# Heads' gate rows of an mLSTM mixer spread over the partitions by a stride-zero transfer in place of a product with a selection column

## The chip, the cores and the metric

The kernel runs on one core of a Trainium2 chip. The metric is the device time of one execution in microseconds (us). TensorE (PE in the profile, PEld its weight loads) multiplies matrices into PSUM; VectorE (DVE), ScalarE (ACT) and GpSimd (POOL) do the rest; SyncE (SP) issues most transfers. SBUF and PSUM have 128 partitions. A time between two kernels is called different here from about 0.2% on.

## The reference, cut to what matters

One layer of a streaming encoder, for a prompt of 2048 tokens and a sample of 64: adaLN and RMSNorm, one input projection, a causal pooling mixer beside an mLSTM with four heads, an output projection, and then a gated MLP. The part that the change touches is the weight matrix of the mLSTM within one chunk of tokens:

```python
b = jnp.cumsum(lf, -1)
dmat = b[..., :, None] - b[..., None, :] + ig[..., None, :]
dmat = jnp.where(causal, dmat, -jnp.inf)
m_t = jnp.maximum(b + m[..., None], dmat.max(-1))
wt = jnp.exp(dmat - m_t[..., None])
a = wt * jnp.einsum('bhtd,bhsd->bhts', q, k)
```

For each head, `wt[t, s]` is the exponential of a term that depends on `t` alone (`b[t] - m[t]`) plus a term that depends on `s` alone (`ig[s] - b[s]`), masked to `s <= t`. The kernel works in chunks of 128 tokens of the prompt (and 64 of the sample).

## The kernel before, in words

The tokens stand in four groups (`groups`, `o.g` 0 to 3) of 512; the last one, `o.last`, also holds the 64 of the sample. For each group the kernel runs the projections of `v` and the gates (`proj_v`), for each of four heads the projections q, k and the output gate (`proj_qko`, 24 matmuls of 512 columns each), four projections for pooling, and the output projection. After the four groups the MLP follows, from about 760 us to the end. Weights are split by ScalarE (line 392) and VectorE (line 395) into a rounded part and a remainder, and each product takes three passes.

The small work between the projections is written as generators. `gemm` calls `tick(0)` after some of its matmuls, which runs the first generator of a list one `yield` further. Two of them matter here. `gate_rows` makes, from the gates, four rows `r` (head by token, on 4 partitions: the term of `t`), a table `R4` and from it, transposed, the columns `CL` (the terms by token on the partition); `drain(0)` in the main loop finishes it before the first `lstm` of the group. `lstm` runs once per head. Its first step builds `at`, the matrix `wt` times the products of k and q:

- line 1274: PE spreads row `hd` of `r` over the partitions, as a product of `E_r[:, hd]` (a selection column, broadcast to 128 columns) with `RHL`. `RHL` holds `r` twice, as a rounded part on partitions 0 to 3 and as the remainder on 32 to 35, since the product reads its operands in a rounded type;
- ScalarE takes the exponential of that PSUM row plus the column of `CL`, four tiles of 128 x 128 into `at`; VectorE clips it by the mask;
- line 1287: PE transposes k, and VectorE multiplies it by a column of `CL` into `kw`;
- line 1297: PE multiplies k and q, and VectorE multiplies `at` by the result.

The second step multiplies `kw` with `va` (line 1312); the third multiplies q with the state (1332) and `at` with `va` (1334).

The order of the instructions on each engine is drawn up by the framework when the kernel is compiled, from the order of the program and simulated times. What is issued through `Urgent` is ranked as if it had been written 200 instructions earlier. `keep_in_program_order` places an instruction behind the one written before it on the same engine. In the profile an instruction issued through `Urgent` has line 231, so that tiles tell more than lines there. Each engine runs its queue in order; a transfer is issued on the queue of an engine, and if it has to wait, what stands behind it waits too. In group 0 VectorE also works through reductions of the conditioning weights (`ada`, line 208).

The kernel already had one transfer of the new kind: `ada` spreads rows of `cs`, in DRAM, over 128 partitions (`s<-cs`, `u<-cs`, `acc<-cs`, line 200), issued by SyncE.

Of the kernel before, what the change touches and what calls it, by code (L numbers as in the profile page):

```python
# [9 lines left out]
F32 = mybir.dt.float32  # L10
F32R = mybir.dt.float32r
# [5 lines left out]
P = 128  # L17
# [23 lines left out]
NH = 4  # L41
# [23 lines left out]
def tile_layer(ctx: ExitStack, tc: tile.TileContext, xT, vecs, cst, rst, w_mod, w_ada, c_rows, w_qkou, w_v, w_pool,  # L65
# [21 lines left out]
    def m2_ps():  # L87
        return bank("m2")
# [34 lines left out]
    def extra():  # L123
        while side:
            try:
                next(side[0])
                return
            except StopIteration:
                side.pop(0)
# [688 lines left out]
    if True:  # L818
# [270 lines left out]
        E_r = a1.tile([P, NH], F32R, tag="E_r", name="E_r")  # L1089
        R4 = a1.tile([P, TMAX], F32, tag="R4", name="R4")  # L1090
        pool.memset(R4, 0.0)
        RHL = a1.tile([P, TMAX], F32R, tag="RHL", name="RHL")
        pool.memset(RHL.bitcast(F32), 0.0)
# [59 lines left out]
        def gate_rows(o, gt, cols):  # L1153
# [55 lines left out]
            act.activation(RHL[0:4, :T], r[:4, :T], AF.Copy)  # L1209
            dve.tensor_tensor(out=RHL[32:36, :T], in0=r[:4, :T], in1=RHL[0:4, :T].bitcast(F32), op=ALU.subtract)  # L1210
            for _ in range(8):
                yield

# [20 lines left out]
            cols += [CL, GL]  # L1234
# [25 lines left out]

        ends = []

        def lstm(o, hd, qko, va, cols, mix):
# [3 lines left out]
            CL, GL = cols  # L1267
            at = a2.tile([P, TMAX], F32, tag="at", name="at")
            kw = a2.tile([P, 5, P], F32, tag="kw", name="kw", bufs=1)
            nd = a2.tile([P, 5, 129], F32, tag="nd", name="nd")  # L1270
            for (a, b, n, s) in o.tsegs:
                lo, w = a * P, (b - a) * n
                pr = m2_ps()
                pe.matmul(pr[:n, :w], E_r[:, hd:hd + 1].broadcast_to([P, n]), RHL[:, lo:lo + w], start=True, stop=True)
                for ti in range(a, b):
                    c0 = (ti - a) * n
                    act.activation(at[:n, ti * P:ti * P + n], pr[:n, c0:c0 + n], AF.Exp, bias=CL[:n, ti, 0, hd:hd + 1])

                av = at[:n, lo:lo + w].rearrange("p (t c) -> p t c", c=n)
                dve.tensor_tensor(out=av, in0=av, in1=mask[:n, :n].unsqueeze(1).broadcast_to([n, b - a, n]), op=ALU.min)  # L1280
# [22 lines left out]
            extra()  # L1303
            yield
# [131 lines left out]
        for o in groups:  # L1436
# [16 lines left out]
            if o.g == 0:  # L1453
                t = scr()
                nc.sync.dma_start(out=t[:P, :NH], in_=cst[:P, NCST + 512:NCST + 512 + NH])
                dve.tensor_copy(E_r, t[:P, :NH])
# [757 lines left out]
def _constants():  # L2214
    c = np.zeros((P, NCST + 512 + NH), np.float32)
# [8 lines left out]
    for h in range(NH):  # L2224
        c[h, NCST + 512 + h] = c[32 + h, NCST + 512 + h] = 1.0
# [71 lines left out]
```

## Time and profile before

| | |
|---|---|
| median of 3 runs | 2172.56 us (2170.78 to 2175.88) |
| the profiled execution | 2170.94 us |
| its span, first to last instruction | 2169.1 us |
| mean granted TensorE clock | 0.998 |
| attention stage | up to about 760 us |
| products of line 1274 | 20, modelled duration 6.6 us in all |
| bytes moved by the transfers | 543.63 MB |

A row of a timeline has the start in us, the us from there to the end of a merged run, the engine, the line, the operation, the tile written and the tiles read, shapes, and the count; brackets at its end give the idle time before it and what ended it. A row of waits has the engine and what it was waiting with, what it waited for, then the total in us, the count and the longest. A row of a table of stretches has the stretch, its length, the busy time and count of PE, its weight loads, VectorE, ScalarE and GpSimd, the granted clock, the share of the transfer engines and GB/s. A row of a transfer has the tile, the queue, the count, KB each and the us from issue to landing. The duration of a matmul is modelled and overlaps the next one; the distance between two starts is what PE spends.

### The profile page before, as it was taken

How to read it: one execution, taken by the hardware profiler on the slowest of the kernel's cores; microseconds unless marked ns; L12 is line 12 of the kernel's file. 1: busy time of each engine (PE TensorE's matmuls, PEld its weight loads, DVE VectorE, ACT ScalarE, POOL GpSimd, SP SyncE). 2: the span in 40 equal slices, each digit the busy share in tenths (PEclk: the TensorE clock that was granted, in tenths of full speed). 3: DMA queues.
4: the chain of work that ended last, by engine and by line, in shares of the span. 5: the costliest groups of instructions: out<-in, count | busy, mean ns of one | idle time of the engine just before them, and what ended most of it. 6: DMA issues, size and time to landing. Idle time of an engine off the chain costs nothing.

```text
span 2169.1 us, 37944 instructions
## 1 busy us (share of the span) xinstructions
PE 2144.5 (99%) x13505; PEld 2041.6 (94%) x13505; DVE 1629.4 (75%) x3068; ACT 1095.8 (51%) x2182; POOL 246.3 (11%) x474
## 2 busy tenths in 40 slices
PE   8999999999999999999999999999999999999998
PEld 7788988888899999999999999999999999999998
DVE  5768769767964768797967668988886597887874
ACT  4455335334333446474636445655655365565554
POOL 0010001001000101010101220100100331111112
PEclk9999999999999999999999999999999999999999
DMA  8897988988886477888967976666668675555542
GB/s 313 305 325 254 348 327 278 344 324 289 279 310 221 155 250 236 290 291 303 346 216 247 322 257 210 233 218 203 224 222 278 221 255 182 175 176 187 175 160 78
DMA packets 245862, 543.63 MB, mean 251 GB/s; under 512 B 25252, under 2 KB 68772, under 8 KB 242856
## 3 DMA queue, kind: packets, MB, share of 16 engines
q1 hardware_dynamic: 236232, 518.89, 70.5%
q10 hardware_dynamic: 9440, 22.32, 2.6%
q8 instruction: 106, 1.74, 0.3%
q14 instruction: 84, 0.69, 0.1%
HBM read 415.12 MB, written 125.99 MB: 249 GB/s over the span
## 4 chain that ended last, share of the span: by engine, by line
PE 83%; DVE 5%; DMA 3%; issue 2%; ACT 1%; SPq 0%; POOL 0%; DVEq 0%; POOLq 0%; ACTq 0%
PE mm L1577 35%; PE mm L458 21%; PE mm L2143 12%; PE mm L2020 8%; PE mm L1122 3%; DVE wt L395 2%; PE m L1312 1%; PE m L1332 1%; PE m L1334 1%; PE m L1297 1%; DMA wt<-wsum 1%; DVE tg L1555 1%; DMA raw<-w_v 1%; DMA raw<-w_ada 0%; ACT tg L1550 0%
## 5 line engine op out<-in xcount | busy, mean ns | idle before, releaser
L1577 PE MATMUL mm<-hx,wt 128*128 128x352 f32 x5544 | 885.2, 321 | 0.8 <-DVE eg L1586 0.5
L1577 PEld LDWEIGHTS mm<-hx,wt 128*128 128x128 f32 x5544 | 878.9, 188 | 1.8 <-DVE wt L395 0.8
L458 PE MATMUL mm<-hl,wt 128*128 128x512 f32 (+2 forms) x1920 | 388.6, 357 | 0.0
L392 ACT ACTIVATE wt<-raw 128x512 fp32r<-128x512 f32 (+3 forms) x470 | 276.5, 597 | 180.6 <-PE mm L2143 49.7
L458 PEld LDWEIGHTS mm<-hl,wt 128*128 128x128 f32 x1920 | 316.3, 189 | 44.3 <-issue 1.1
L395 DVE TENSOR_TENSOR wt<-raw,wt 128x512 fp32r<-128x512 f32 (+3 forms) x470 | 312.7, 671 | 57.3 <-ACT wt L392 57.1
L2143 PE MATMUL mm<-av,wt 128*128 128x448 f32 (+1 forms) x1632 | 262.7, 322 | 0.0
L2143 PEld LDWEIGHTS mm<-av,wt 128*128 128x128 f32 x1632 | 250.4, 188 | 11.1
L1992 DVE SCALAR_TENSOR_TENSOR x<-mm,MOD,x 128x352 f32<-128x352 f32 (+3 forms) x360 | 167.5, 505 | 78.4 <-PE mm L2143 65.0
L2020 PE MATMUL mm<-av,wt 128*128 128x352 f32 x1344 | 220.8, 323 | 2.3 <-DVE x L1992 0.7
L2020 PEld LDWEIGHTS mm<-av,wt 128*128 128x128 f32 x1344 | 215.4, 188 | 5.4 <-DVE ea L1586 3.4
L1624 ACT ACTIVATE mm<-mm 128x352 f32<-128x352 f32 x196 | 87.8, 448 | 250.9 <-PE mm L1577 194.5
L458 PE MATMUL mm<-mx,wt 128*128 128x512 f32 (+1 forms) x960 | 183.1, 352 | 0.6 <-DVE scr L231 0.6
L458 PEld LDWEIGHTS mm<-mx,wt 128*128 128x128 f32 x960 | 159.4, 188 | 23.5 <-DVE scr L231 0.5
L1555 DVE SCALAR_TENSOR_TENSOR ta<-ea,V,ta 128x704 f32<-128x704 f32 (+1 forms) x132 | 125.7, 952 | 64.3 <-ACT ta L1550 51.9
L1555 DVE SCALAR_TENSOR_TENSOR tg<-eg,V,tg 128x704 f32<-128x704 f32 (+1 forms) x132 | 125.7, 953 | 59.9 <-ACT tg L1550 57.5
L395 DVE TENSOR_TENSOR wt<-wt 128x512 fp32r<-128x512 f32 x196 | 132.9, 684 | 12.8 <-ACT wt L392 12.7
L392 ACT ACTIVATE wt<-wt 128x512 fp32r<-128x512 f32 x196 | 120.1, 623 | 30.7 <-DMA wt<-wsum 25.4
L1764 ACT ACTIVATE tg<-tg 128x704 f32<-128x704 f32 (+1 forms) x66 | 52.4, 795 | 70.9 <-DVE tg L1555 70.9
L1533 POOL COPY ea<-UC 128x2 f32<-128x2 f32 x66 | 32.9, 498 | 483.4 <-DVE ta L1555 398.2
L1122 PE MATMUL mm<-wt,hl 128*128 128x256 f32 (+1 forms) x576 | 71.3, 284 | 0.0
L1122 PEld LDWEIGHTS mm<-wt,hl 128*128 128x128 f32 x576 | 70.4, 190 | 0.8 <-issue 0.6
(292 smaller groups left out, 2175.1 us busy)
## 6 DMA issues: line engine op xcount, KB each, us to landing
wt<-wsplit SPq DMA_DIRECT2D x132, 512.0 KB, 4.4
raw<-w_up SPq DMA_DIRECT2D x198, 256.0 KB, 4.1
wt<-hl_kept SPq DMA_DIRECT2D x96, 512.0 KB, 5.8
wt<-wsum SPq DMA_DIRECT2D x132, 256.0 KB, 5.0
wsplit<-wt SPq DMA_DIRECT2D x66, 512.0 KB, 5.8
w<-w_up SPq DMA_DIRECT2D x44, 512.0 KB, 5.8
wsum<-w SPq DMA_DIRECT2D x22, 1024.0 KB, 4.9
Bd<-fscr ACTq DMA_DIRECT2D x56, 352.0 KB, 4.3
```

The costliest lines, as they stand in the source:

```text
L392: act.activation(u.w[:, 0, :u.n], u.raw[:, :u.n], AF.Copy)
L395: dve.tensor_tensor(out=u.w[:, 1, :u.n], in0=u.raw[:, :u.n], in1=u.w[:, 0, :u.n].bitcast(F32), op=ALU.subtract)
L458: pe.matmul(ps[bi][:, :hi - lo], U[:, a, k % 4 * P:(k % 4 + 1) * P], mv[k][:, b, lo:hi], start=(at == 0 and pi == 0), stop=(k == order[-1] ...
L1122: pe.matmul(ps[ti][:n, :cols], h[4 * kh + k4][:, b, lo:lo + n], U[:, a, k4 % 2 * cols:(k4 % 2 + 1) * cols], start=(kh == 0 and k4 == 0 and ...
L1533: pool.tensor_copy(ext[:, 0:2], UC[:, f, :])
L1555: dve.scalar_tensor_tensor(out=t[:, :E], in0=ext[:, j:j + E], scalar=wc(j, f), in1=t[:, :E], op0=ALU.mult, op1=ALU.add)
L1577: pe.matmul(bk.t[:, :FH], U[:, a, kc * P:(kc + 1) * P], Bo.at(nm, kc, b), start=(first and kc == 0 and pi == 0), stop=(kc == 3 and pi == 2 ...
L1624: act.activation(to.t[:, :FH], bk.t[:, :FH], AF.Copy)
L1764: act.activation(self.tg[:, :E], self.tg[:, :E], AF.Silu)
L1992: dve.scalar_tensor_tensor(out=x3[n][:, a:b], in0=bk.t[:, a - lo:b - lo], scalar=gt2(n, s), in1=x3[n][:, a:b], op0=ALU.mult, op1=ALU.add)
L2020: pe.matmul(bk.t[:, :FH], U[:, a, c:c + P], quad.put(op, m, b), start=(first and m == 0 and pi == 0), stop=(m == 1 and pi == 2), skip_grou ...
L2143: pe.matmul(bks[i].t[:, :hi - lo], U[:, a, k % 4 * P:(k % 4 + 1) * P], av[k][:, b, lo:hi], start=(k == 0 and (a, b) == PASSES[0]), stop=(k ...
```

## The change

The rows `r` are written to DRAM by one transfer for each group (`rd`, from ScalarE's queue), eight `yield`s later the first head's row is read back with a stride of zero over the partitions straight into `at`, and the next head's row is read at the end of the first step of each head's `lstm`. The exponential then works in place on `at`, held behind the ScalarE instruction written before it. The product, `E_r` with its small load and copy, and `RHL` with its copy, its subtraction and its memset go.

```diff
-        E_r = a1.tile([P, NH], F32R, tag="E_r", name="E_r")
         R4 = a1.tile([P, TMAX], F32, tag="R4", name="R4")
         pool.memset(R4, 0.0)
-        RHL = a1.tile([P, TMAX], F32R, tag="RHL", name="RHL")
-        pool.memset(RHL.bitcast(F32), 0.0)
...
             yield
-            act.activation(RHL[0:4, :T], r[:4, :T], AF.Copy)
-            dve.tensor_tensor(out=RHL[32:36, :T], in0=r[:4, :T], in1=RHL[0:4, :T].bitcast(F32), op=ALU.subtract)
+            rd = dr.tile([4, TMAX], F32, tag=f"rd{o.g}", name=f"rd{o.g}")
+            act.dma_start(out=rd[:, :T], in_=r[:4, :T])
             for _ in range(8):
                 yield
+            spread = [at_tile(o, rd, 0)]
...
-            cols += [CL, GL]
+            cols += [CL, GL, rd, spread]
...
+        def at_tile(o, rd, hd):
+
+            t = a2.tile([P, TMAX], F32, tag="at", name="at")
+            Urgent(nc.scalar).dma_start(out=t[:, :o.T], in_=rd[hd:hd + 1, :o.T].broadcast_to([P, o.T]))
+            return t
...
         def lstm(o, hd, qko, va, cols, mix):
...
-            CL, GL = cols
-            at = a2.tile([P, TMAX], F32, tag="at", name="at")
+            CL, GL, rd, spread = cols
+            at = spread.pop()
...
-                pr = m2_ps()
-                pe.matmul(pr[:n, :w], E_r[:, hd:hd + 1].broadcast_to([P, n]), RHL[:, lo:lo + w], start=True, stop=True)
                 for ti in range(a, b):
-                    c0 = (ti - a) * n
-                    act.activation(at[:n, ti * P:ti * P + n], pr[:n, c0:c0 + n], AF.Exp, bias=CL[:n, ti, 0, hd:hd + 1])
+                    cell = at[:n, ti * P:ti * P + n]
+                    tc.keep_in_program_order(act.activation(cell, cell, AF.Exp, bias=CL[:n, ti, 0, hd:hd + 1]))
...
             extra()
+            if hd < NH - 1:
+                spread.append(at_tile(o, rd, hd + 1))
             yield
...
-            if o.g == 0:
-                t = scr()
-                nc.sync.dma_start(out=t[:P, :NH], in_=cst[:P, NCST + 512:NCST + 512 + NH])
-                dve.tensor_copy(E_r, t[:P, :NH])
```

The constants `cst` lose the four selection columns. The product's bank of PSUM, one of those that `m2_ps` hands out in turn, is no longer taken.

More of the change, by code (lines that the diff above doesn't have):

```diff
@@ L2214, in _constants @@
 def _constants():
-    c = np.zeros((P, NCST + 512 + NH), np.float32)
+    c = np.zeros((P, NCST + 512), np.float32)
     c[127, C_L127:C_L127 + P] = 1.0
@@ L2223, in _constants @@
     c[:, NCST:NCST + 512] = np.tile(m, (1, 4))
-    for h in range(NH):
-        c[h, NCST + 512 + h] = c[32 + h, NCST + 512 + h] = 1.0
     return c
```

## The prediction

> **What bounds the kernel now.** I read the summary first: which engine is full, at what clock, and whether the transfers have room.
>
> ```profile
> span 2169.1 us, 37944 instructions
> PE 2144.5 (99%) x13505; PEld 2041.6 (94%) x13505; DVE 1629.4 (75%) x3068; ACT 1095.8 (51%) x2182; POOL 246.3 (11%) x474
> DMA  8897988988886477888967976666668675555542
> PE 83%; DVE 5%; DMA 3%; issue 2%; ACT 1%; SPq 0%; POOL 0%; DVEq 0%; POOLq 0%; ACTq 0%
> ```
>
> PE is busy 99% of the span and carries 83% of the chain that ended last. So whatever leaves PE's queue should leave the time, and whatever leaves another engine should not, except where PE waits for that engine. The transfers are busy 8 to 9 tenths in the first thirteen slices, which are the attention stage where the change lies; that is room, but not much.
>
> Second, who makes PE wait, in the attention stage from 70 us to 760 us:
>
> ```profile
> PE m L1312 <- DVE kw L231: 3.8, 2, 3.0
> PE mm L1366 <- DVE nd L231: 2.1, 2, 1.4
> PE m L1165 <- DVE gt L231: 0.9, 1, 0.9
> PE mm L458 <- DVE scr L231: 0.6, 2, 0.3
> PE m L885 <- DMA w<-w_out: 0.2, 1, 0.2
> ```
>
> The columns are total, times, longest. That is all: 7.6 us in 690. One wait of 3.0 us stands out, for `kw`, which is built in the same step of `lstm` that the change touches. The others are below 1.5 us. So the stage is PE's own time plus one visible hole.
>
> **What the change removes on PE.** The tile view of the rows' product says how many there are, and the timeline what one costs:
>
> ```profile
> L1274 PE MATMUL m<-RHL,E_r x20: 196/395/483, 73.5 to 704.4; 128*128 128x512 f32 x16, 128*64 128x64 f32 x4
> 260.95 0.40 PE L1274 MATMUL m<-RHL,E_r 128*128 128x512 f32 x1
> 261.18 0.60 PE L1287 MATMUL m<-V,k 128*128 128x128 f32 x4
> 625.10 0.43 PE L1274 MATMUL m<-RHL,E_r 128*128 128x512 f32 x2
> 625.37 0.88 PE L458 MATMUL mm<-hl,wt 128*128 128x256 f32 x5
> ```
>
> The duration of 0.40 us is not the price, since matmuls overlap: the next product starts 261.18 - 260.95 = 0.23 us later. In the last group a 512-wide and a 64-wide one together take 625.37 - 625.10 = 0.27 us, so the narrow one costs 0.04. Sixteen and four: 16 x 0.23 + 4 x 0.04 = 3.84 us, if PE is the limit at each of the twenty. That is the case at fifteen of the sixteen heads as far as the waits show (15 x 0.23 + 4 x 0.04 = 3.6 us). The exception is the first head of group 0.
>
> **The first head of group 0.** There VectorE, not PE, sets the pace:
>
> ```profile
> 65.86 0.68 DVE L231 TENSOR_TENSOR RHL<-scr,RHL 4x512 fp32r<-4x512 f32 x1
> 66.57 0.69 DVE L395 TENSOR_TENSOR wt<-raw,wt 128x512 fp32r<-128x512 f32 x1
> ...
> 74.03 0.63 ACT L392 ACTIVATE wt<-raw 128x512 fp32r<-128x512 f32 x1 [3.05 <-DMA raw<-w_qkou]
> 74.69 0.69 DVE L395 TENSOR_TENSOR wt<-raw,wt 128x512 fp32r<-128x512 f32 x1 [0.52 <-ACT wt L392]
> ...
> 75.04 1.14 ACT L231 ACTIVATE at<-m,CL 128x128 f32<-128x128 f32 x4
> ...
> 78.19 0.69 DVE L231 TENSOR_TENSOR at<-at,mask 128x512 f32<-128x512 f32 x1
> 78.80 0.68 DVE L231 TENSOR_TENSOR kw<-m,CL 128x512 f32<-128x512 f32 x1
> 79.40 0.68 DVE L231 TENSOR_TENSOR at<-at,m 128x512 f32<-128x512 f32 x1
> 79.63 0.57 PE L1312 MATMUL m<-va,kw 128*128 128x129 f32 x3 [2.95 <-DVE kw L231]
> ```
>
> VectorE runs without a break here, works through reductions of L208 until 78.19, then the mask, then `kw`, and PE stands 2.95 us. Removing a product ahead of a hole only makes the hole longer, so the sixteenth product is worth nothing by itself. What VectorE loses is the subtraction at 65.86, which holds it for 66.57 - 65.86 = 0.71 us. But at 74.69 it waits 0.52 us for ScalarE's `wt`, which itself waited 3.05 us for a weight transfer; so of those 0.71 us perhaps nothing arrives. The other end: the subtraction's time arrives whole, and `kw` passes ahead of the mask (78.80 - 78.19 = 0.61 us), together 1.3 us. Below nothing: the new 256 KB transfer of this head delays that weight transfer. I take a gain of 0.4 us, nearer to the row at 74.69, with ends of -1.3 and +0.65 (the latter from the next part).
>
> **What it adds on the transfers.** Each group writes its four rows to DRAM (4 x 2 KB), and each head reads one row back 128 times (256 KB; 288 KB in the last group). Both shapes have neighbours:
>
> ```profile
> cs<-gap SPq DMA_DIRECT2D x1, 8.0 KB, 3.4
> s<-cs SPq DMA_DIRECT2D x8, 256.0 KB, 4.7
> L813 ACTq DMA_DIRECT2D Bd<-fscr x56: 326/326/348, 884.0 to 1631.0; - x56
> 72.00:76.00 4.00, 4.00 (x25) 3.47 (x24) 3.48 (x10) 1.97 (x6) 0.00 (x0) 1.00 0.91 315
> 84.00:88.00 4.00, 4.00 (x24) 3.47 (x23) 2.87 (x10) 1.11 (x4) 0.00 (x0) 1.00 1.06 409
> 63.82 0.63 ACT L231 ACTIVATE RHL<-scr 4x512 fp32r<-4x512 f32 x1 [0.66 <-DVE scr L231]
> 242.82 0.63 ACT L231 ACTIVATE RHL<-scr 4x512 fp32r<-4x512 f32 x1 [0.25 <-DVE scr L231]
> 248.04 0.60 ACT L1240 ACTIVATE q<-mm 128x512 f32<-128x512 f32 x1 [4.32 <-PE mm L458]
> 261.38 1.14 ACT L231 ACTIVATE at<-m,CL 128x128 f32<-128x128 f32 x4 [1.01 <-PE m L1274]
> 282.03 1.14 ACT L231 ACTIVATE at<-m,CL 128x128 f32<-128x128 f32 x4 [0.99 <-PE m L1274]
> ```
>
> `s<-cs` is the same thing that the change introduces: one DRAM row of 512 values spread over 128 partitions, 4.7 us from issue to landing; an issue from ScalarE takes its queue 0.33 us. The chain from the rows to the first head's exponential becomes 0.33 + 3.4 + 0.33 + 4.7 = 8.8 us. In the trace there are 75.0 - 63.8 = 11.2 us between the two in group 0 and 261.4 - 242.8 = 18.6 us in group 1, so it fits, in group 0 with 2.4 us to spare. The tiles of heads 1 to 3 are asked for one head ahead, some 20 us before their use (the exponentials of group 1's first two heads start at 261.38 and 282.03). Cover holds; if that of group 0 fails, the exponential waits on ScalarE's in-order queue, and the mask, `kw` and PE behind it, microsecond for microsecond.
>
> The bytes: 12 x 256 + 4 x 288 KB = 4.3 MB in all. At the 409 GB/s that the full engines show (the last two columns are their share and rate) one 256 KB tile takes 0.65 us of all sixteen engines; that is the +0.65 above. In other places I cost it at nothing: PE waited for weights nowhere in the stage, and the units are fetched several ahead.
>
> **What it adds and removes on ScalarE.** It adds 20 issues, 20 x 0.33 = 6.6 us, and removes four copies of 0.63 us; the exponentials (0.29 us each in a run of four) read SBUF in place of PSUM, whose cost I take as equal, bounded by the 0.63 us of a 512-wide copy from SBUF against 0.60 from PSUM for such an evacuation (within 5%). ScalarE is busy 51% and no row of PE's waits names it, so +4 us there are costed at nothing. Two waits are new on its queue. The first spread waits until the rows have landed; queued behind it are the splits `wt` of coming weights and evacuations. The exponentials are now held behind whatever ScalarE instruction was written just before, as a rule a weight split, which may wait for a transfer; in the trace above they stood behind that split (74.03) anyway. VectorE gets rid of 4 x 0.7 us, off the path outside group 0.
>
> **The sum.** 3.6 + 0.4 = 4.0 us less. Ends: the three lesser waits for `kw` (3.8 - 3.0 = 0.8) and `nd` (twice) swallow the three products ahead of them, 0.7 us, and the first head costs 0.65: 3.6 - 0.7 - 0.65 = 2.2 us less. The other way 3.6 + 1.3 = 4.9 less. The profiled execution took 2170.94 us, of which 2169.1 are the span; it would come to 2166.9. It lies 1.6 us under the median of 2172.56 us, from which the forecast is 2168.6. A measurement of this kernel can tell about 0.2%, 4.35 us, from no change: the forecast lies just inside.
>
> **Rivals.** *The hole closes.* The order of VectorE's work is drawn up anew, and the exponentials no longer depend on PE. If the mask and `kw` come up before the reductions, the hole of 2.95 us goes, and something with it:
>
> ```profile
> 76.40:79.60 3.20, 0.28 (x2) 0.00 (x1) 3.16 (x9) 0.63 (x1) 0.00 (x0) 1.00 0.98 362
> 80.30:83.70 3.40, 3.40 (x12) 2.84 (x11) 2.98 (x8) 0.63 (x1) 0.00 (x0) 0.50 1.05 405
> 83.70:87.00 3.30, 3.30 (x21) 2.87 (x21) 2.17 (x7) 1.11 (x4) 0.00 (x0) 1.00 1.05 405
> 256.00:260.00 4.00, 4.00 (x20) 3.35 (x19) 0.20 (x2) 0.55 (x4) 1.01 (x1) 1.00 0.98 397
> ```
>
> (PE, its weight loads, VectorE, ScalarE and GpSimd, then the granted clock, transfers, GB/s.) Right after the hole the granted clock is 0.50 for 3.4 us (12 products there, against 21 in the 3.30 us after): 1.7 us lost. With both gone the sum is 3.6 + 2.95 + 0.23 + 1.7 = 8.5 us less, 2164.1. For it speaks that ScalarE was done with the exponentials at 76.2, two microseconds before the mask began; against it that these reductions stood ahead for other reasons than the removed product. The Trainium skill (TensorE: Matmul & The Clock Gate, Part 1) says that an idle window of about 3.4 us puts the array at half clock, by a window that runs free of the kernel. The trace agrees in the 3.4 us at 0.50, though a hole of 2.95 us sufficed, and by that rule the loss would come and go between executions.
>
> *ScalarE is held.* The first spread is issued too early and ScalarE stands until the rows have landed, 3.4 us. In group 0 the splits behind it reach VectorE late and the hole grows by up to that: 3.6 - 3.4 gives 2172.4, no change. From group 1 on VectorE has gaps to absorb it, as in the last row above: busy 0.20 of 4 us ahead of the first head. Against it: eight steps of the generator are left between write and spread, and 11.2 us. The Trainium skill (DMA: Bandwidth & Descriptors, the anatomy of one DMA) states that a transfer's wait is served on the issuing queue before dispatch; no row here shows such a wait on ScalarE yet.
>
> *The transfers become the bound*, the case on the other side. All sixteen tiles fall into stretches where the engines are full, weights come late, and PE stands for each: 16 x 0.65 = 10.4 us, less 3.6, gives +6.8 or 2179.4. It decides from 3.6 / 16 = 0.23 us of PE's time for each tile. For it: shares of 0.91 to 1.06 around 80 us, and ScalarE's own wait of 3.05 us for a weight transfer. Against it: no wait of PE for `wt` in 690 us, so the prefetch has a margin that 0.65 us at a time should not use up.
>
> **How the numbers follow.** The forecast's case gets 0.45, with a range of its own of 2167.7 to 2170.4, so 0.15 of it lies beyond the 4.35 us and 0.30 within; the closing hole, whole or in part, 0.25; ScalarE held 0.18; transfers 0.12. Faster is 0.15 + 0.25 = 0.40, the same 0.30 + 0.18 = 0.48, slower 0.12. The range runs from 2163.5, just under the closed hole, to 2176.5, where partial contention would put it; beyond lie most of the 0.12 and a little of the 0.25.
>
> **What would show it.** Right: the twenty products of L1274 gone, and the span 4 us shorter, though PE's modelled busy time falls by more (0.40 us for each); PE's waits for `kw` still one of 2 to 3 us in group 0; sixteen spreads landing in 4 to 6 us. Wrong: a wait of ScalarE for the row transfer of over 1 us, PE waiting for `wt`, or no hole and no half clock at 76 us, or new holes at other heads because the order of an engine was drawn up differently.

## The result, and the profile after

The kernel after takes 2175.76 us (median of 20 runs, 2173.10 to 2179.04), the kernel before 2172.56 us beside it (20 runs). The ratio is 1.0015, with a 95% interval of 1.0009 to 1.0022: 3.2 us slower. That is less than the 0.2% which counts as different here, but the forecast was 4 us the other way, and the interval excludes no change.

The summary of the profile after, as it was read before: the span, the engines, the transfers' share in 40 slices, the chain that ended last.

```profile
span 2174.2 us, 37930 instructions
PE 2144.2 (99%) x13485; PEld 2039.8 (94%) x13485; DVE 1625.7 (75%) x3063; ACT 1094.4 (50%) x2178; POOL 246.8 (11%) x473
DMA  8898998998887477888967976666668675555552
PE 74%; DVE 7%; DMA 2%; issue 2%; ACT 1%; DVEq 0%; POOL 0%; SPq 0%; POOLq 0%; ACTq 0%
```

The 20 products are gone, yet the span is 5.1 us longer. One profile alone proves little of that size: the stretch behind the last projection of the stage, the same program in all kernels, took 1433.8 us here, and 1437.1 in a kernel that runs the same order of instructions (the last row of the table below). PE's share of the chain fell from 83% to 74%, and VectorE's rose from 5% to 7%: PE waits at more places. Its waits from 70 to 760 us:

```profile
PE m L1316 <- DVE kw L231: 6.7, 3, 3.6
PE mm L1370 <- DVE nd L231: 1.8, 2, 0.9
PE mm L458 <- ACT CL L231: 1.6, 1, 1.6
PE m L1338 <- DVE at L231: 0.3, 1, 0.3
```

The wait for `kw` grew from 3.8 us at two places to 6.7 at three, and one of 1.6 us put down to `CL` is new. What is behind them shows in SyncE's waits, 60 to 760 us:

```profile
SPq L195 <- DMA at<-rd: 3.9, 1, 3.9
SPq L376 <- DMA rd<-scr: 3.5, 1, 3.5
SPq L853 <- DMA at<-rd: 2.3, 1, 2.3
SPq L376 <- DMA at<-rd: 2.1, 2, 1.3
```

These are transfers of weights (`raw<-w_ada`, `wt<-hl_kept`, `wsum<-w`) that read and write nothing of `rd` or `at`. The trace lists with each transfer the semaphore that it raises when it has landed. SyncE's and ScalarE's transfers take the same eight in turn, and a transfer isn't issued before the last one with its semaphore has landed: the rows' write at 425.09 and the weight that SyncE issues at 430.12 both raise number 103. In this way a slow transfer of ScalarE holds an unrelated one of SyncE: 3.9 + 3.5 + 2.3 + 2.1 = 11.8 us in all, none of it before.

**Group 2, where the loss is easiest to read.** The chain of work that ended last in the stretch from 425 to 448 us, in order of time (start, us, what):

```profile
425.09 4.96 DMA rd<-scr
...
430.08 0.34 ACTq L231
...
430.46 6.64 DMA at<-rd
...
437.58 6.24 DMA raw<-w_ada
...
443.85 0.75 DVE junk L208
...
446.07 0.62 DVE kw L231
...
446.83 1.13 PE m L1316 x8
```

No matmul bounds this stretch. The rows' write takes 4.96 us to land. Then ScalarE issues the spread, and head 1's right behind it (430.46), which lands after 6.64. Then SyncE issues the transfers that waited for it, a conditioning weight among them; that lands 6.24 us later, VectorE reduces it, and `kw` stands behind this reduction. (The reductions of line 208 run in the later groups too, not in group 0 alone.) The same from SyncE, VectorE and PE in the timeline, one fence each:

```profile
426.19 0.33 SPq L195 DMA_DIRECT2D raw<-w_ada  x1
430.12 0.81 SPq L376 DMA_DIRECT2D wt<-hl_kept  x2
430.98 4.75 SPq L195 DMA_DIRECT2D raw<-w_ada  x2
```

```profile
438.18 0.75 DVE L208 CUSTOM_DVE_ANT_0 junk<-raw,u,V 128x512 f32<-128x512 f32 x1 [3.92 <-DMA raw<-w_ada]
```

```profile
435.63 5.02 PE L458 MATMUL mm<-hl,wt 128*128 128x512 f32 x21 [1.58 <-ACT CL L231]
446.83 0.35 PE L1316 MATMUL m<-va,kw 128*128 128x129 f32 x1 [1.19 <-DVE kw L231]
```

SyncE stands from 426.5 to 430.12, for the write, and again between the two of the merged row from 430.98, for a spread. VectorE stands 3.92 us for the conditioning weight. PE stands 1.58 and 1.19 us. The first of these the profile puts down to `CL`; but the instruction waits there for the semaphore of `wt<-hl_kept`, the weight that SyncE could issue only at 430.12 and that landed at 435.50. So both are SyncE's held transfers.

**Where the change won.** I compared the start of each projection matmul with that of the same matmul in a kernel without the transfers (the first experiment). From the start of group 3 to its end the kernel before falls behind by 6.22 - 4.95 = 1.3 us, the kernel after by nothing (10.58 at both ends). In group 2 the kernel before falls behind by 0.9. There PE's price of 0.23 us for a product was right. In group 1 it gains 0.7 us up to the last head and has lost that again at the end of the group, since the kernel without transfers has a new wait of 1.3 us there. In group 0 it falls behind by 4.0, of which four products are 0.9; the rest is a longer hole (3.0 us against 2.2), other waits, and the 3.4 us at half clock behind the hole, which the trace without transfers doesn't have.

### The profile page after: what moved, and what is told of

It reads as the page before. It is cut to its first block, busy times and chain, and to the rows that moved or that the text cites. A ratio compares the mean times of both kernels' runs of the same rounds, so it can differ in the third digit from the quotient of the medians.

```text
span 2174.2 us, 37930 instructions
## 1 busy us (share of the span) xinstructions
PE 2144.2 (99%) x13485; PEld 2039.8 (94%) x13485; DVE 1625.7 (75%) x3063; ACT 1094.4 (50%) x2178; POOL 246.8 (11%) x473
## 4 chain that ended last, share of the span: by engine, by line
PE 74%; DVE 7%; DMA 2%; issue 2%; ACT 1%; DVEq 0%; POOL 0%; SPq 0%; POOLq 0%; ACTq 0%
PE mm L1577 36%; PE mm L458 14%; PE mm L2143 12%; PE mm L2020 8%; DVE wt L395 2%; PE mm L1119 1%; DVE tg L1555 1%; DMA raw<-w_ada 1%; PE m L1316 1%; PE m L1336 1%; PE m L1338 1%; DVE scr L231 0%; PE m L1299 0%; ACT tg L1550 0%; DMA Bd<-fscr 0%
## 5 line engine op out<-in xcount | busy, mean ns | idle before, releaser
L392 ACT ACTIVATE wt<-raw 128x512 fp32r<-128x512 f32 (+3 forms) x470 | 276.7, 597 | 167.8 <-PE mm L2143 49.3
```

Of the source, the lines that this page charges most:

```text
L392: act.activation(u.w[:, 0, :u.n], u.raw[:, :u.n], AF.Copy)
```

## The experiments

Three theories were put down ahead of them. H: queues are held, ScalarE's by the spread that waits for the rows and SyncE's by the semaphores. B: the bytes, that is, the spreads lie in front of weights in full stretches. O: the drawn order of the engines' work is worse. Each ratio is to runs of the kernel before on the same chip.

| run | ratio to before | 95% interval |
|---|---|---|
| no transfers, the product gone | 0.9981 | 0.9972 to 0.9990 |
| transfers kept, the product back | 1.0041 | 1.0028 to 1.0053 |
| spreads of a constant row, no write | 1.0010 | 1.0001 to 1.0019 |
| spreads in program order | 1.0005 | 0.9996 to 1.0014 |
| all on GpSimd's queue | 1.0011 | 1.0002 to 1.0020 |
| all on GpSimd's queue, spreads in program order | 1.0018 | 1.0009 to 1.0027 |
| transfers in groups 1 to 3 | 1.0012 | 1.0003 to 1.0021 |
| the same on GpSimd's queue; again | 1.0004; 1.0017 | 0.9994 to 1.0014; 1.0008 to 1.0025 |
| the same, spreads in program order | 1.0002 | 0.9993 to 1.0010 |
| groups 2 and 3, ScalarE's queue | 1.0010 | 1.0001 to 1.0018 |
| groups 2 and 3, GpSimd's queue | 0.9998 | 0.9988 to 1.0008 |
| the same, spreads doubled | 1.0009 | 1.0001 to 1.0018 |
| groups 2 and 3, write ScalarE, spreads GpSimd | 1.0000 | 0.9991 to 1.0009 |
| groups 2 and 3, write GpSimd, spreads ScalarE | 0.9997 | 0.9987 to 1.0006 |
| group 1 alone | 1.0006 | 0.9996 to 1.0015 |
| group 0 alone | 1.0008 | 0.9999 to 1.0017 |
| after with a hold on VectorE in group 1 | 1.0014 | 1.0004 to 1.0024 |

**Transfers away, and product back.** The first kernel has neither write nor spreads:

```diff
-            rd = dr.tile([4, TMAX], F32, tag=f"rd{o.g}", name=f"rd{o.g}")
-            act.dma_start(out=rd[:, :T], in_=r[:4, :T])
+            rd = rst
...
-            Urgent(nc.scalar).dma_start(out=t[:, :o.T], in_=rd[hd:hd + 1, :o.T].broadcast_to([P, o.T]))
...
-                    tc.keep_in_program_order(act.activation(cell, cell, AF.Exp, bias=CL[:n, ti, 0, hd:hd + 1]))
+                    tc.keep_in_program_order(act.activation(cell, mask[:n, :n], AF.Exp, scale=0.0, bias=CL[:n, ti, 0, hd:hd + 1]))
```

> The changed kernel with neither the write nor the spreads: the exponentials read a constant tile with scale 0, so this leaves out the gate term of the token t. The product stays removed. H and B: what the transfers cost is gone, 2168 to 2170, the removed 3.8 us show in full. O: the order of VectorE is what costs, so 2173 to 2177, with waits for kw as in after.

The second keeps all transfers and puts the product (with `E_r` and `RHL`) back behind them:

```diff
+                pr = m2_ps()
+                pe.matmul(pr[:n, :w], E_r[:, hd:hd + 1].broadcast_to([P, n]), RHL[:, lo:lo + w], start=True, stop=True)
...
-                    cell = at[:n, ti * P:ti * P + n]
-                    tc.keep_in_program_order(act.activation(cell, cell, AF.Exp, bias=CL[:n, ti, 0, hd:hd + 1]))
+                    c0 = (ti - a) * n
+                    act.activation(at[:n, ti * P:ti * P + n], pr[:n, c0:c0 + n], AF.Exp, bias=CL[:n, ti, 0, hd:hd + 1])
```

> The kernel after with one part undone: the product on PE, with its selection column and its rounded rows, is back and the exponentials read it from PSUM, while the rows' write and the sixteen spreads stay as they are; each spread lands in the tile that the exponentials then overwrite. This closes the square: the transfers with the product. Additive costs, whatever their cause (theory H, held queues, and theory B, bytes): the transfers cost what lies between the kernel without them and the kernel after, 1.0015 - 0.9981 = 0.34% or 7.4 us, so this kernel is 7.4 us slower than the kernel before, some 2179.5 us where before has 2172. A reading in which the transfers only hurt because the exponentials read them: no slower than the kernel after, +3 us. If the removed product hid part of the holds, less than 7.4 us but more than 3.

Measured: 0.9981 without transfers, 4.1 us faster (2.2 to 6.1), the forecast's 4.0; 1.0041 with both, 8.9 us slower (6.1 to 11.5). So without the transfers the change is worth about 4 us, though not where the forecast put them: by the comparison above 4.0 of the 6.2 us in the stage come from group 0 and its clock, and none from group 1. The transfers cost 1.0015 - 0.9981 = 0.34% or 7.4 us without the product beside them, 8.9 with it; what they do to the drawn order and to the clock is counted in. Theory O, the removed product alone, falls as the cause of the whole. PE's waits, 70 to 760 us, without transfers:

```profile
PE m L1314 <- DVE kw L231: 3.5, 2, 2.2
PE mm L1368 <- DVE nd L231: 1.0, 2, 0.6
PE mm L458 <- DVE scr L231: 0.3, 1, 0.3
```

Even here one wait for `kw` (1.3 us, in group 1) is new against before, and the one in group 0 is shorter, 2.2 us against 3.0. That much the drawn order changes by itself, both ways.

**The same bytes, without waiting for rows.** `rd = rst`, a constant input, with the spreads as they were.

> The changed kernel without the write of the rows: each spread reads a row of the input rst in place of the group's own row, so this leaves out the gate term of the token t, and no spread waits for a write. Bytes of the spreads, ScalarE's issues and the place of the exponentials stay. Theory H (held queues: the spread waits on ScalarE's queue for the write to land, 4.4 to 5.0 us in the trace of after, and SyncE's later transfers wait behind the completion of the row write and of the spreads, 11.8 us in all): the holds on ScalarE and those of SyncE on the row write go, 2169 to 2172, with SyncE's waits on the write at 0 and on the spreads under 3 us. Theory B (bytes: 4.3 MB more make weights late): 2175 to 2177 as after. Theory O (order: with the product gone, VectorE's work is drawn up in a worse order, mask ahead of kw and reductions ahead of both): 2174 to 2177, with the waits for kw at the first head of group 2 and the second of group 1 still there.

Measured 1.0010, but at another place. With nothing to wait for, two of group 0's spreads were issued at 26.3 and 28.7 us, among loads at the kernel's start, and the first projection starts 6.6 us late, behind 6.8 us at half clock. From group 1 on it lost at most 0.4 us against the kernel without transfers, in one profile. So twelve tiles need cost no more than that where they are free to move; that the same bytes were dear at the start because they lay in front of something that was due is argued, not shown.

**The other way to issue.** In one run the spreads stand in program order, in one all transfers are on GpSimd's queue:

```diff
-            Urgent(nc.scalar).dma_start(out=t[:, :o.T], in_=rd[hd:hd + 1, :o.T].broadcast_to([P, o.T]))
+            tc.keep_in_program_order(nc.scalar.dma_start(out=t[:, :o.T], in_=rd[hd:hd + 1, :o.T].broadcast_to([P, o.T])))
```

> The changed kernel with the spreads held behind the ScalarE instruction written before them instead of ranked 200 instructions earlier: the spread of head 1 is no longer issued together with that of head 0, and each is issued later. Computes everything. H: fewer transfers stand waiting while SyncE's go by, the hold on the row write gets shorter, 2170 to 2174. B: 2175 to 2177. O: 2174 to 2177.

```diff
-            act.dma_start(out=rd[:, :T], in_=r[:4, :T])
+            Urgent(nc.gpsimd).dma_start(out=rd[:, :T], in_=r[:4, :T])
...
-            Urgent(nc.scalar).dma_start(out=t[:, :o.T], in_=rd[hd:hd + 1, :o.T].broadcast_to([P, o.T]))
+            Urgent(nc.gpsimd).dma_start(out=t[:, :o.T], in_=rd[hd:hd + 1, :o.T].broadcast_to([P, o.T]))
```

> The changed kernel with the write and the spreads issued by GpSimd (11% busy) instead of ScalarE: same bytes, but neither ScalarE's queue nor the completion semaphores that SyncE's transfers take in turn are used. Computes everything. H: 2168 to 2171, no wait of SyncE on the rows or spreads; a loss only if GpSimd's small powers are held behind a spread. B: 2175 to 2177. O: 2174 to 2177.

In program order: 1.0005, and SyncE still waits for rows and spreads. On GpSimd's queue: 1.0011. There SyncE waits for none of them and groups 2 and 3 lose nothing against the kernel without transfers, as H says; but group 1 loses 4.1 us (with 3.4 us at half clock, which the kernel after doesn't have there) and group 0 4.6, as the kernel before does (4.0). So there are at least two mechanisms, in different groups. Both in one (on GpSimd's queue and in program order) was to beat both kernels:

> The kernel after with all its transfers on GpSimd's queue and the spreads in program order: one tile at a time in every group, no queue of ScalarE or SyncE held. It is the candidate for a version that beats both. In the profiles, spreads in program order from ScalarE's queue lost 3.8 us in group 0 against the kernel without transfers, as the kernel before does (4.0), and 0.6, 1.2 and 0.8 us in the others, the latter two by held queues. So 0.6 us in group 1 and nothing in 2 and 3 here: about 2.5 us faster than before, ratio 0.9988, if holds and pairs of tiles are the whole loss. If it stays at 1.000 or above, something else takes the product's 3.7 us.

It didn't: 1.0018. In its profile groups 0 and 1 lose 5.6 and 4.6 us, with 6.8 and 3.4 us at half clock in them.

**Groups 2 and 3: the queue alone.** The product stays in groups 0 and 1; the two kernels differ in nothing but the engine that issues. Up to 450 us the traces of these two, and of the next two, have the same order of instructions on PE, VectorE and SyncE, so the drawn order isn't what differs in group 2.

```diff
+            if o.g < 2:
+                rd, spread = None, []
+                act.activation(RHL[0:4, :T], r[:4, :T], AF.Copy)
+                dve.tensor_tensor(out=RHL[32:36, :T], in0=r[:4, :T], in1=RHL[0:4, :T].bitcast(F32), op=ALU.subtract)
+            else:
+                rd = dr.tile([4, TMAX], F32, tag=f"rd{o.g}", name=f"rd{o.g}")
+                Urgent(nc.gpsimd).dma_start(out=rd[:, :T], in_=r[:4, :T])
```

> The product kept in groups 0 and 1, in which VectorE also works through the conditioning weights' reductions; rows and spreads, issued by GpSimd, in groups 2 and 3 only. Eight products leave PE, 8 x 0.23 + 0.04 x 2 = 1.9 us. Theory H: nothing holds ScalarE or SyncE and the loss of these two groups on GpSimd's queue was 0.4 us or less, so 1.5 to 1.9 us faster than before, ratio 0.9991 to 0.9993, and the fastest correct form of the change tried so far. Theory B in its strong form, 0.65 us for each of eight tiles wherever they fall: 5.2 - 1.9 = 3.3 us slower.

> As the kernel with the product kept in groups 0 and 1 and transfers in groups 2 and 3, but these are issued from ScalarE's queue, as in the kernel after, in place of GpSimd's. Same bytes, same groups, same product: the queue alone differs. Theory H (held queues): group 2 loses 3.9 to 4.7 us as in the kernel after and in the one with the product in group 0 alone, SyncE waits for rows and spreads by 5 us or more, and the time is some 4 us above the kernel on GpSimd's queue, 2 to 3.5 us above before, ratio 1.0009 to 1.0016. Theory B (bytes): as on GpSimd's queue, 0.9993 to 0.9998.

GpSimd's queue 0.9998, ScalarE's 1.0010. The intervals overlap, and a repeat (below) differed by as much; the profiles are apart. PE's only wait from 415 us to the end of the stage on GpSimd's queue:

```profile
PE mm L458 <- DVE scr L231: 0.9, 2, 0.6
```

On ScalarE's queue, SyncE's waits from 415 to 450 us, and then the timeline of ScalarE, VectorE and PE:

```profile
SPq L376 <- DMA at<-rd: 5.2, 2, 3.9
SPq L376 <- DMA rd<-scr: 4.5, 1, 4.5
```

```profile
428.59 0.60 ACT L1247 ACTIVATE q<-mm 128x512 f32<-128x512 f32 x1 [4.30 <-DMA rd<-scr]
...
441.50 0.75 DVE L208 CUSTOM_DVE_ANT_0 junk<-raw,u,V 128x512 f32<-128x512 f32 x1 [4.36 <-DMA raw<-w_ada]
...
445.83 1.41 PE L1331 MATMUL m<-va,kw 128*128 128x129 f32 x5 [3.82 <-DVE kw L231]
```

SyncE held, a late conditioning weight, a late reduction, and PE stands 3.82 us for `kw`, with 6.8 us at half clock behind it. By the comparison of starts group 2 loses 6.9 us here and nothing on GpSimd's queue. The other profiles agree: in five kernels with write and spreads on ScalarE's queue, the spreads ranked ahead, group 2 loses 2.9 to 6.9 us; in four with the same on GpSimd's queue, each spread once, it loses nothing. Theory H holds for group 2.

It names two holds, ScalarE's and SyncE's. Write and spreads on different queues tell them apart:

> Product in groups 0 and 1, transfers in groups 2 and 3; the rows' write from ScalarE's queue, the spreads from GpSimd's. ScalarE waits for nothing, since a write needs no landed rows; SyncE may wait for the write by its completion semaphore, 4.5 us once, as in the run with both on ScalarE. If ScalarE's stand before the first spread, or SyncE's behind the spreads, made group 2's loss: none here, ratio as with both on GpSimd, 0.9998, and no wait for kw above 1 us after 416 us. If SyncE's wait for the write alone is enough: kw late in group 2 by 1 to 4 us, ratio 1.0005 to 1.0010.

> The other half: product in groups 0 and 1; the rows' write from GpSimd's queue, the spreads from ScalarE's. ScalarE stands until the rows have landed, 4 to 5 us in each of two groups, if the first spread is still issued right behind the write; SyncE waits for spreads, 7 us or so, not for the write. If these two make the loss: kw late in group 2 by 2 to 4 us, ratio 1.0010 as with both on ScalarE. If the write's semaphore was the cause: 0.9998.

The first measured 1.0000: SyncE waited 5.6 us for the write, and PE lost nothing. Then the second was to lose as much as both together (1.0010), and it measured 0.9997. ScalarE and PE in its timeline:

```profile
427.28 0.60 ACT L1247 ACTIVATE q<-mm 128x512 f32<-128x512 f32 x1 [6.86 <-DMA rd<-scr]
...
441.01 1.13 PE L1331 MATMUL m<-va,kw 128*128 128x129 f32 x8 [0.98 <-DVE kw L231]
```

ScalarE stood 6.86 us for the rows, longest of all, and PE lost 1 us. So ScalarE's stand by itself isn't what costs: what is queued behind it isn't due. What is left is SyncE. It was held 5.6 us behind the write alone and 6.2 us behind the spreads alone, and 8 to 10 us behind the one and then the other in the five kernels that lose; either alone was nearly covered by what is fetched ahead. Whether ScalarE's stand adds to the loss where SyncE is held by both was not tried.

Bytes where no queue is held, by issuing each of the eight spreads twice (the line of the spread on GpSimd's queue stands twice):

> As the kernel with the product in groups 0 and 1 and transfers from GpSimd's queue in groups 2 and 3, but each of these eight spreads is made twice into the same tile: 8 x 0.25 to 0.28 MB more. It prices bytes where no queue of ScalarE or SyncE is held. Theory B: 0.65 us for each tile more, 5.2 us above the kernel with single spreads, ratio 1.002. Theory H: no PE wait is added outside the profile's noise, ratio as with single spreads, 0.9993 to 0.9998.

1.0009 against 0.9998 with single spreads: 0.11%, 2.4 us for eight more tiles, 0.3 us each, where B said 0.65 and H nothing. The intervals overlap, and by the comparison of starts the doubled kernel loses 2.5 us in these groups, the single one 0.2, but another with single spreads lost 1.4 in group 3 alone. So a price of the bytes by themselves, about half of B's, is possible and not shown.

**Groups 0 and 1.** The product kept in group 0, with ScalarE's and with GpSimd's queue in groups 1 to 3, and with the spreads in program order; the diffs are those above with `o.g == 0` for `o.g < 2`:

> The kernel after, but group 0 keeps the product as in the kernel before, with neither rows' write nor spreads; groups 1 to 3 as in the kernel after. Twelve products leave PE, 12 x 0.23 + 3 x 0.04 = 2.9 us. Theory B (two 256 KB tiles in front of the weight transfers where the transfer engines are full, so in group 0): all of the loss is gone, 2.9 us faster than before, ratio 0.9987. Theory H (ScalarE's queue held until the rows have landed, SyncE's by the completion semaphores that both take in turn): groups 1 to 3 keep their losses, read from the profiles against the kernel without transfers as 1.7, 3.6 and 0.1 us, so 2.5 us slower than before at most and about equal at least, ratio 1.000 to 1.001, with waits of SyncE for the rows or the spreads of 8 us or more in all.

> As the kernel with the product kept in group 0, but in groups 1 to 3 the rows' write and the spreads are issued by GpSimd. Theory H: SyncE waits for none of them and groups 2 and 3 lose nothing; group 1 lost 4.1 us in the profile of the kernel that moved all of them to GpSimd, because VectorE stood 3.86 us in a reduction waiting for a conditioning weight ahead of the head's own work. If that came of group 0's delay, it is gone here and the kernel is 2.9 us faster than before (0.9987); if it came of the order drawn for VectorE, it stays and the kernel is about 1 us slower (1.0005). Theory B: as the kernel with the product in group 0, the queue makes no difference.

> As the kernel with the product in group 0 and transfers from GpSimd's queue in groups 1 to 3, but the spreads stand in program order and not hoisted: head 1's no longer beside head 0's, 20 us later. The order of the other engines is the same. If two tiles in front of the 1 MB transfer made group 1's 3.9 us (theory B there): 1 us or less is left, the kernel is 2 to 2.9 us faster than before, ratio 0.9987 to 0.9991. If the order drawn for VectorE and SyncE made them: 3 us or more stay, ratio about 1.001.

1.0012, then 1.0004, then 1.0002. The first is H's number. The second stays where the drawn order or the bytes were to leave it: group 1 loses 3.9 us by the comparison of starts. In program order, so that head 1's spread no longer stands beside head 0's, it loses 2.3, between the 1 us of theory B there and the 3 of the order. But PE's waits from 240 to 340 us are the same in both kernels:

```profile
PE m L1331 <- DVE kw L231: 1.9, 1, 1.9
PE m L1353 <- DVE at L231: 1.0, 1, 1.0
PE m L1351 <- DVE st L231: 0.2, 1, 0.2
```

What differs is the clock in the 3.4 us behind the wait for `kw`, in the first and then in the one in program order:

```profile
287.80:291.20 3.40, 3.40 (x12) 3.04 (x13) 2.79 (x7) 0.63 (x1) 0.00 (x0) 0.51 1.01 418
```

```profile
286.00:289.40 3.40, 3.08 (x18) 2.69 (x18) 3.21 (x8) 0.64 (x1) 0.00 (x0) 1.00 0.99 406
```

So moving head 1's tile away took nothing off PE's waits, and the 1.6 us are the half clock. VectorE in group 1, without transfers and in the kernel after:

```profile
260.21 0.75 DVE L208 CUSTOM_DVE_ANT_0 junk<-raw,u,V 128x512 f32<-128x512 f32 x1 [1.33 <-DMA raw<-w_ada]
279.94 0.69 DVE L231 TENSOR_TENSOR at<-at,mask 128x512 f32<-128x512 f32 x1
280.55 0.68 DVE L231 TENSOR_TENSOR kw<-m,CL 128x512 f32<-128x512 f32 x1
```

```profile
267.10 0.75 DVE L208 CUSTOM_DVE_ANT_0 junk<-raw,u,V 128x512 f32<-128x512 f32 x1 [2.90 <-DMA raw<-w_ada]
286.90 0.69 DVE L231 TENSOR_TENSOR at<-at,mask 128x512 f32<-128x512 f32 x1
287.50 0.68 DVE L231 TENSOR_TENSOR kw<-m,CL 128x512 f32<-128x512 f32 x1
```

In both the redrawn order has a reduction stand for its weight in the middle of head 0's step, and head 1's mask ahead of its `kw`; in the kernel before `kw` (282.82) came ahead of the mask (283.42). The transfers make that weight 1.6 us later still. Two kernels were to move the reduction behind head 0's step by a hold:

```diff
-                dve.tensor_tensor(out=at[:n, lo:lo + w], in0=at[:n, lo:lo + w], in1=pq[:n, :w], op=ALU.mult)
+                i = dve.tensor_tensor(out=at[:n, lo:lo + w], in0=at[:n, lo:lo + w], in1=pq[:n, :w], op=ALU.mult)
+                if o.g == 1:
+                    tc.keep_in_program_order(i)
```

> As the kernel with the product in group 0 and transfers from GpSimd's queue in groups 1 to 3, but in group 1 the product of at with the scores is held on VectorE behind kw, so that no reduction that waits for a conditioning weight stands between them. If the order drawn for VectorE made group 1's 3.9 us (theory O, in its group), they go, and the kernel is the fastest of the correct ones: 12 x 0.23 + 3 x 0.04 = 2.9 us faster than before, ratio 0.9987. If they come from transfers that landed late because the two spreads lay in front of a 1 MB one (theory B there), only the 1.0 us at the first head goes and 2 us at the second stay: ratio about 1.000.

> The kernel after with one hold added: in group 1 the product of at with the scores is held on VectorE behind kw, so that the reduction that stood 2.9 us for a conditioning weight comes behind it. In the profile of the kernel after, group 1 lost 0.8 us at the first head and 2.0 us at the second while VectorE worked off the delay. If the drawn order of VectorE made them: 2 to 2.8 us less than the kernel after, ratio 1.0002 to 1.0006. If the late weight transfers made them (theory H by the semaphores, theory B), only 0.8 us go and the ratio stays above 1.001.

The hold changed nothing: the drawn order of VectorE came out the same, since a hold behind `kw` doesn't keep a reduction from standing between. So the two are repeats of kernels above, the first of 1.0004 (it gave 1.0017, a measure of what an interval here can miss), the second of the kernel after (1.0014). The order's part in group 1 shows in the kernel that keeps the transfers and has the product back. VectorE's order in this group is there that of the kernel before, and PE waits nowhere in the group, as in the kernel before. With the product gone, PE waits for `kw` at head 1: 1.3 us without transfers, and 1.9 to 2.0 us in all ten kernels whose spreads wait for their rows, whatever the queue. So in group 1 the hole comes with the redrawn order, and the transfers lengthen it.

Last, the transfers in one group alone, as in the kernel after:

> Transfers as in the kernel after in group 1 alone, the product as before in groups 0, 2 and 3. Four products leave PE, 0.9 us. In the profiles, group 1 went from 0.7 us won (the kernel before) to 1.7 us lost (after) against the kernel without transfers, so 2.4 us slower than before, ratio 1.0011. The part of it that the redrawn order makes: the kernel without transfers has a hole of 1.5 us for kw there that the kernel before has not. If a group loses only together with the late starts of the group ahead of it: the 0.9 us are won, ratio 0.9996.

> Transfers as in the kernel after in group 0 alone, the product as before in groups 1 to 3. In the profiles, group 0 stood at 4.0 us (before) and 4.4 us (after) against the kernel without transfers, with a half clock of 3.4 us in the one and 6.8 us in the other, which differs between executions of one program. So 0.4 us slower, ratio 1.0002, that is nothing measurable; two tiles in front of the weight transfers eat what three or four products bring. If the longer half clock always follows: 1.4 us more, 1.0008.

1.0006 and 1.0008, with 1.0010 for groups 2 and 3 (above): 1.3, 1.7 and 2.2 us, 5.2 in all where the kernel after has 3.2, each uncertain by 2. No group brings a win, and no single one the loss.

In group 0 the transfers are 2 x 0.65 us of tiles in front of a weight. ScalarE's split of that weight without transfers, and in the kernel after, whose first projection starts 0.97 us later:

```profile
72.42 0.63 ACT L392 ACTIVATE wt<-raw 128x512 fp32r<-128x512 f32 x1 [1.42 <-DMA raw<-w_qkou]
```

```profile
74.70 0.63 ACT L392 ACTIVATE wt<-raw 128x512 fp32r<-128x512 f32 x1 [2.72 <-DMA raw<-w_qkou]
```

74.70 - 72.42 - 0.97 = 1.31 us later, about the two tiles. The hole for `kw` is 3.61 us in the kernel after, and behind it the clock is half for 6.8 us:

```profile
80.00:83.40 3.40, 2.50 (x10) 2.44 (x11) 3.38 (x9) 1.02 (x2) 0.00 (x0) 0.50 1.03 405
83.40:86.80 3.40, 3.40 (x9) 2.63 (x9) 2.99 (x10) 0.00 (x0) 0.00 (x0) 0.50 1.06 407
```

That isn't the transfers' doing alone: in the eleven kernels that keep the product and no transfer in group 0, the half clock there lasts nothing, 3.4 or 6.8 us, and the group loses 2.8 to 6.1 us; in the six with transfers in place of the product and waiting for rows, 3.6 to 5.6. So the profiles don't show a price of the transfers in group 0.

## Why the prediction was wrong

- **What PE gets rid of** was right as a price: 0.23 us a product shows in groups 2 and 3. That the total without transfers, 4.1 us, is also the forecast's 4.0 is partly luck: group 1 won nothing, because the order was redrawn, and group 0 won more than its products, with a shorter hole and no half clock in that profile.
- **The step that failed** is the price of the transfers outside group 0: "In other places I cost it at nothing: PE waited for weights nowhere in the stage, and the units are fetched several ahead." Measured, the transfers cost 7.4 us, where the sum's ends had 0.65. In groups 1 to 3 alone the sum is missed by 5.5 us, uncertain by 2: 1.0012 is 2.6 us slower where their twelve wide products and the narrow ones should have made 2.9 us faster. In group 2 it is the held transfers, 2.9 to 6.9 us by the profiles; in group 1 it is a hole for `kw` of 1.9 us that came with the redrawn order, which the prediction had among its signs and gave no price. PE's list of waits was the wrong witness. PE doesn't wait for a conditioning weight, VectorE does, and what PE shows is a wait for `kw`. VectorE's own waits for these weights were what I had to read: 8.5 us at eight places in the trace of before from 60 to 760 us, and 16.7 at ten in that of after.
- **"+4 us there are costed at nothing. Two waits are new on its queue."** That is ScalarE's. The waits were named and then given no price outside a rival. ScalarE did stand for the rows, and the run with the write on GpSimd's queue and the spreads on ScalarE's shows that this costs little by itself; the rival *ScalarE is held* had the wait and the wrong victim. Its "VectorE has gaps to absorb it" failed too: the gap in its row was a wait for PE's `GL` (2.96 us), and in group 2 the hold made VectorE stand 3.92 us for a conditioning weight ahead of `kw`. The rows were taken to land in 3.4 us, and took 4.96 in group 2.
- **SyncE's queue** is missing from the step: that a transfer of ScalarE holds SyncE's later ones by a shared semaphore. In group 2 this is the loss, 6.9 us in the worst profile, half clock included.
- **"The tiles of heads 1 to 3 are asked for one head ahead"** failed for head 1. The spread is written at the end of head 0's step, but `Urgent` ranks it 200 instructions earlier, and it was issued beside head 0's in all four groups. So group 0 has two tiles in front of its weights, 1.3 us where the range's end had 0.65, and the first head's hole grew from 2.95 to 3.61 us where the sum took a gain of 0.4.
- **The range's upper part** was *the transfers become the bound*, 0.65 us for each tile. Not so: without a wait for rows twelve tiles cost 0.4 us by one profile, and eight more on GpSimd's queue measured 2.4 us, which the uncertainty doesn't tell from nothing. (The shares of the transfers in the first thirteen slices run from 6 to 9 tenths, not 8 to 9 as read.)
- **Left open:** what in the transfers lengthens group 1's hole from 1.3 to 1.9 us, what they cost in group 0, and whether the three kernels that lose little in groups 2 and 3 are faster. Their profiles show 1.0 to 1.9 us won in these groups, where eight products should bring 1.9. Their ratios have a mean of 0.9998, 0.4 us, and each interval reaches 2 us or more the fast way, so they tell neither. No kernel with the transfers was measurably faster than the kernel before.

## What to carry to other kernels

An instruction taken off the full engine pays only if what replaces it is free on every queue it passes: for a transfer its bytes, the engine that stands until its source has landed, and the transfers on other queues that wait for its completion semaphore. Before you cost one at nothing, read the waits of the queues and of the engine behind the full one, not only those of the full one. Where an instruction is ranked ahead of its place, look up in the drawn order where it will come. And where the order is drawn anew, an instruction that goes can cost by what takes its place: in group 1 the hole came with the product's removal, not with the transfers.

## What the runs showed of the hardware

The half clock doesn't follow from the hole alone. Two of the kernels above have the same drawn order: transfers in groups 1 to 3 on GpSimd's queue, without and with the hold that changed nothing. Group 0's hole in the timeline and the 3.4 us behind it in the table of stretches, for the first and then for the second:

```profile
79.76 2.06 PE L1331 MATMUL m<-va,kw 128*128 128x129 f32 x8 [2.48 <-DVE kw L231]
```

```profile
79.60:83.00 3.40, 3.24 (x12) 2.98 (x13) 2.70 (x7) 0.63 (x1) 0.00 (x0) 0.50 1.02 371
```

```profile
79.72 1.13 PE L1333 MATMUL m<-va,kw 128*128 128x129 f32 x8 [2.47 <-DVE kw L231]
```

```profile
79.60:83.00 3.40, 3.28 (x19) 2.88 (x19) 2.91 (x6) 0.72 (x2) 0.00 (x0) 1.00 1.04 409
```

One execution ran at 0.50 behind 2.48 us, the other at full clock behind 2.47. In the stage the half clock came in pieces of 3.4 or 6.8 us in all profiles. The Trainium skill (TensorE: Matmul & The Clock Gate, Part 1) has a window of about 3.4 us that runs free of the kernel and makes the cost vary between runs. The traces agree with that, and with the length; its rule that an idle window of about 3.4 us is needed isn't borne out by a hole of 2.48.

What decides can be worked out from the twenty traces. Within each trace the clock changed only at multiples of 3.413 us from its first change. Of these windows up to 760 us, at full clock, all 24 in which PE was busy (as modelled) for less than 43.7% were followed by half clock, none of those above 49.3%, and three of the ten between. (At the kernel's very end windows of 43 to 71% were followed by it; why isn't known.) In the pair above the hole took PE down to 32% in one window of the first; in the second a boundary split it, 54% and 74%. So the same hole costs clock or not by where the windows fall.

The write of 8 KB to DRAM took 4.96 us to land in group 2, against 3.4 for a like one in the trace of before. The Trainium skill (DMA: Bandwidth & Descriptors, the anatomy of one DMA) gives a fixed cost of about 2 us for a transfer that GpSimd issues and says that a wait is served by the issuing queue before dispatch. The second is what the row at 428.59 shows (4.30 us behind a spread that waits); the first is well under what was seen on ScalarE's queue.
